# One layer's attention written out in a recorded order on all five engines, with the row minima of grouped-query attention scaled on ScalarE

## The chip, the cores and the metric

The kernel runs on one core of a Trainium2 chip. The metric is device time in microseconds (us) of one execution, from its first to its last instruction. The time before is 1951.8 us, the median of three runs (1947.15 to 1954.22).

## The reference

A two-layer diffusion backbone works on 512 latent and 256 context tokens of 1024 channels. Each layer normalises and modulates the tokens, projects them, attends in two branches, adds the gated branches, projects again, and ends with a SwiGLU feed-forward block. The part around the change is the attention:

```python
na_q, na_k, na_v, gq, gk, gv, ga, gb = jnp.split(h @ w_in[l], IN_SPLITS, axis=-1)
ya = merge_heads(na_latent(qa, ka, va, ka_c, va_c, bias, row_idx))   # 8 heads, 8x16 window + context
qb = apply_rope(rms_norm(heads(gq, GQA_Q_HEADS), q_gain[l]), cos, sin)   # 8 query heads
kb = apply_rope(rms_norm(heads(gk, GQA_KV_HEADS), k_gain[l]), cos, sin)  # 2 key heads
ob = gqa_latent(qb, k_all, v_all)     # softmax over 512 latent + 256 context keys
x = x + g1 * branch_merge(ya, yb, ga, gb, w_pa[l], w_pb[l], w_o[l])
if not last: ...                      # the context tokens' own queries, in layer 0 only
```

## The kernel before, in words

Every large product is done in full precision as three products of rounded halves: a weight or activation is cast to a high part on ScalarE (`wh`, L369) and its rest is taken on GpSimd or VectorE (`wl`, L371), and TensorE adds high x high, high x low and low x high in one PSUM bank (L384).

The attention of one layer is built by `mixing`. Its items are pairs of query blocks: per head two pairs of 128 queries, 16 pairs of grouped-query attention (`gqa_pair`) and then 16 of windowed attention (`na_pair`). For a grouped-query pair, TensorE writes the scores of two blocks into three PSUM banks (`sc`, L1040), VectorE takes each row's minimum (L1048; the scores carry a minus sign) and multiplies it by the query's inverse norm (L1054), ScalarE takes the exponential with that value as bias (`p`, L1056), VectorE divides by the row sums (L1009, L1010), TensorE transposes (`tp`, L1066), ScalarE and VectorE split the transposed block into halves (`pth` L1016, `ptl` L1017), and TensorE multiplies with the values (`y`, L1076), whose two partition halves are joined by ScalarE and VectorE (L1024, L1027). The scores have one set of three banks, the transposes and values three banks (`t`), the projections two (`g`). So the next pair's scores wait until this pair's exponentials have read theirs.

Between the items TensorE runs fillers: the projections of later heads, with their evacuation (`gqa_q`, `na_k`, `na_q`, `na_v`, `gate`). `Flow` plans this. It keeps a clock, books each evacuation or exponential on a line per engine (`go`, with fixed and per-element costs in `RATE`), and lets a filler run where an item would have to wait. The table `PLAN` holds one row of settings for each layer. What `Flow` decides is TensorE's order alone: the loop runs under a manual schedule for PE, and the order on VectorE, ScalarE, GpSimd and SyncE is set by the framework's scheduler.

Layer 1 starts its attention with the latent tokens while the context tokens are still being normalised (`late_norm`, `late_k`, `late_v`): the keys come in a latent part of 512 and a context part of 256 columns, and the first scores need both (`kk`, L1352 and L1353). GpSimd does the inverse norms (L807, a power), one product of the rotary embedding (L791), most of the `wl` and the windowed bias (L1491, L1492). SyncE loads the weights (L360) and moves query halves across partitions (L1001).

Of the kernel before, what the change touches and what calls it, by code (L numbers as in the profile page):

```python
# [44 lines left out]
for _n in ORDER:  # L45
    for _j in range(COLS[_n][1]):
# [32 lines left out]
         busy=12, ctx=0.0, vat=(1, 1), load=2, qt=2, rx=2, slow=(1.1, 1.2, 1), banks="gst", lead=(2, 1, 2), quiet=0.0, spared=0),  # L79
# [3 lines left out]
         busy=2, ctx=1, vat=(1, 1), load=2.5, qt=2, rx=1, slow=(1, 1, 1), banks="tsg", lead=(2, 2, 1), quiet=28.0, spared=2),  # L83
# [42 lines left out]


# [20 lines left out]
class Flow:  # L148
# [4 lines left out]
    def __init__(self, fillers, live, pace, hop, slow):  # L153
# [10 lines left out]

        self.rings = dict(g=[0.0] * 2, t=[0.0] * 3)
# [37 lines left out]
    def fill(self):  # L203
# [4 lines left out]
        if f.state == 0:  # L208
            next(f.steps)
# [4 lines left out]
        try:  # L214
            v = next(f.steps)
        except StopIteration:
# [8 lines left out]
        else:  # L225
            self.clock += v
# [5 lines left out]
    def ahead(self):  # L232

        for f in self.fillers:
            if f.state == 1:
                return
            if f.state == 0:
                next(f.steps)
                f.state = 1
                return  # L240

# [10 lines left out]
    def run(self, steps):  # L252
        mine = 0.0
        self.ahead()
        for v in steps:
            if isinstance(v, Until):
                self.wait(v.t)
            else:
                self.clock += v
# [8 lines left out]
    def force(self, ready):  # L268
        while not ready():
            if not self.fill():  # L270
                self.rest(self.clock + 0.5)

# [62 lines left out]
class Trunk:  # L335
    def __init__(self, tc, nc, dram):
        self.tc, self.nc, self.d = tc, nc, dram
# [12 lines left out]
    def ps(self, tag, n="ps", cols=512):  # L350
        if tag not in self.pbufs:
            tag = "a" if tag == "g" else "t" if "t" in self.pbufs else "n"
        return self.psum[tag].tile([P, cols], F32, tag=tag, bufs=self.pbufs[tag], name=self.name(n))
# [467 lines left out]
    def gqa_k(self, l, h, spans, pool, out):  # L821
# [25 lines left out]
        end = self.roped(flow.clock + 0.7)  # L847
        self.rope(kg, pool)
# [45 lines left out]
    def gqa_q(self, l, j, h, spans, pool, out):  # L894
# [14 lines left out]
        end = max(end, self.roped(flow.clock - 1.0))  # L909
        nr = self.small.tile([P, 16], F32, tag="hr", name=self.name("nr"))  # L910
        nc.vector.tensor_scalar(nr[:, : n // HD], r[:, : n // HD], -1.0, None, op0=ALU.mult)
        self.rope(qg, pool)
        yield Until(end - self.plan["soon"])
# [116 lines left out]
    def gqa_pair(self, head, q, kk, val, out, i, pool, done=None):  # L1030
# [20 lines left out]
        def exp(s, b, at):  # L1051
            m = ms[b]
            c = 2 * b + v
            nc.vector.tensor_tensor(m[:, 0:1], m[:, 0:1], r[:, c : c + 1], op=ALU.mult)  # L1054
# [4 lines left out]
            end = self.go(("v", 1), ("e", T), at=at)  # L1059
# [27 lines left out]
    def ctx_item(self, head, score, val, out, r, nr, v, pool, done):  # L1087
# [4 lines left out]
        def soft(s, at):  # L1092
# [3 lines left out]
            if r is not None:  # L1096
                rr = r[:].rearrange("p (t v) -> p v t", v=2)[:, v, 4:6]
                nc.vector.tensor_tensor(m[:, 0:2], m[:, 0:2], rr, op=ALU.mult)
            p = pool.tile([P, 512], F32, tag="p", name=self.name("p"))
            for b in range(2):  # L1100
# [4 lines left out]
                self.soften(p[:, c], m[:, 2 + b : 3 + b], pool)  # L1105
            ps_.append(p)
            end = self.go(("v", S), ("v", 1), ("e", 256), ("e", 256), at=at)
            return end, self.go(("v", 1), ("v", 1), ("w", 256), ("w", 256), at=end - 0.5)
# [45 lines left out]
    def na_pair(self, head, q, k, val, bias, out, i, pool, done=None):  # L1154
# [16 lines left out]
        def soft(s, b, at):  # L1171
# [7 lines left out]
                halves(z[:]), halves(s[:, 0:512]), add, 1.0, BIG, ALU.add, ALU.min, m[:, 0:1])  # L1179
            nc.scalar.activation(z, z, AF.Exp, bias=m[:, 0:1], scale=-1.0, accum_out=m[:, 1:2])  # L1180
            self.soften(z, m[:, 1:2], pool)
            zs.append(z)
            free = self.go(("v", S), at=at)
# [126 lines left out]
    def late_k(self, l, h, pool, out):  # L1310
# [7 lines left out]
        for a, b in ((0, S), (S, T)):  # L1318
# [22 lines left out]
            if a == 0:  # L1341
                end = self.roped(flow.clock + 0.7)
# [1015 lines left out]
```

## Time and profile before

| what | value |
|---|---|
| median of three runs | 1951.8 us (1947.15, 1951.8, 1954.22) |
| the profiled execution: its own time, its span | 1945.29 us, 1943.5 us |
| busy share of the span: PE, VectorE, ScalarE, GpSimd | 98%, 76%, 49%, 12% |
| mean granted TensorE clock | 0.998 |
| layer 0's attention, about 100 to 420 us | PE busy 316.8 of 320 us |
| layer 1's attention, about 1150 to 1400 us | PE busy 239.9, VectorE 196.4, ScalarE 153.4, GpSimd 67.2 of 250 us |

A row of the timeline gives the start, the time, the engine, the line, the operation with what it writes and reads, and in square brackets how long the engine stood idle before it and who ended that. PE is TensorE, DVE VectorE, ACT ScalarE, POOL GpSimd, SP SyncE. Busy time of PE overlaps from matmul to matmul, so its idle time is a little larger than what the busy share leaves.

### The profile page before, as it was taken

What the parts mean: (1) busy time and instruction counts of PE and PEld (TensorE: products, weight loads), DVE (VectorE), ACT (ScalarE), POOL (GpSimd) and SP (SyncE); (2) the same over time, 40 slices, a digit from 0 to 9 for tenths busy, and PEclk for the clock granted to TensorE, in tenths of its full rate; (3) what the DMA queues carried; (4) which work ended last, traced back from release to release, by engine and by line L of the source; (5) the groups of instructions that cost most, each with busy time, mean ns of one, the idle gap of its engine ahead of it and who ended that gap; (6) DMA issues with size and microseconds to landing.
All of it is one profiled execution on the core that took longest, in us unless ns stands there. A gap on an engine that the chain in (4) does not pass through costs nothing.

```text
span 1943.5 us, 31493 instructions
## 1 busy us (share of the span) xinstructions
PE 1912.1 (98%) x12298; PEld 1775.8 (91%) x12298; DVE 1470.0 (76%) x2802; ACT 943.0 (49%) x1822; POOL 226.6 (12%) x131
## 2 busy tenths in 40 slices
PE   8999999999999999999999998999999999999998
PEld 8989999998899999999999888889988999999998
DVE  7468887769877888786868577888657687877785
ACT  5466666652336533342424346666553355544553
POOL 0332222213300000000000012322300000000000
PEclk9999999999999999999999999999999999999999
DMA  8121112235562233334344411112235532332332
GB/s 328 44 65 48 47 64 63 77 105 182 170 217 87 66 120 122 117 116 133 131 141 143 143 62 55 47 60 64 73 102 173 201 109 77 98 120 88 103 97 83
DMA packets 71669, 210.85 MB, mean 108 GB/s; under 512 B 8544, under 2 KB 10720, under 8 KB 71520
## 3 DMA queue, kind: packets, MB, share of 16 engines
q1 hardware_dynamic: 71520, 208.84, 33.5%
q8 instruction: 96, 1.57, 0.3%
q14 instruction: 53, 0.43, 0.1%
HBM read 196.75 MB, written 6.82 MB: 105 GB/s over the span
## 4 chain that ended last, share of the span: by engine, by line
PE 69%; DVE 4%; issue 1%; ACT 1%; POOL 0%; DMA 0%; DVEq 0%; POOLq 0%; ACTq 0%
PE po L384 21%; PE qu L1740 14%; PE pj L384 11%; PE qv L1740 7%; PE pp L384 4%; PE qc L1740 3%; PE pf L384 3%; PE pv L957 1%; PE sc L1040 1%; PE y L1076 1%; PE tp L1066 1%; PE y L1203 1%; PE sc L1167 1%; PE tp L1191 1%; DVE m L1048 0%
## 5 line engine op out<-in xcount | busy, mean ns | idle before, releaser
L1740 PE MATMUL qu<-r,w 128*128 128x384 f32 (+1 forms) x1872 | 295.9, 310 | 0.3
L1740 PEld LDWEIGHTS qu<-r,w 128*128 128x128 f32 x1872 | 281.0, 190 | 4.9 <-DVE tt L2219 3.7
L384 PE MATMUL pj<-h,wh 128*128 128x512 f32 (+1 forms) x704 | 257.4, 366 | 3.3 <-ACT kg L816 1.7
L384 PE MATMUL pj<-h,wl 128*128 128x512 f32 (+1 forms) x704 | 247.6, 352 | 1.2 <-POOL wl L371 1.2
L384 PE MATMUL pj<-hl,wh 128*128 128x512 f32 (+1 forms) x704 | 247.0, 351 | 0.0
L369 ACT ACTIVATE wh<-wr 128x1024 fp32r<-128x1024 f32 (+1 forms) x131 | 124.6, 954 | 168.9 <-issue 43.5
L1603 ACT ACTIVATE w<-wr 128x512 fp32r<-128x512 f32 x234 | 145.4, 625 | 107.6 <-DVE wr L2183 36.1
L384 PE MATMUL po<-ph,wh 128*128 128x512 f32 (+1 forms) x576 | 197.5, 343 | 0.0
L384 PE MATMUL po<-ph,wl 128*128 128x512 f32 (+1 forms) x576 | 196.9, 342 | 0.0
L384 PE MATMUL po<-pl,wh 128*128 128x512 f32 (+1 forms) x576 | 196.3, 341 | 0.0
L371 POOL TENSOR_TENSOR wl<-wr,wh 128x1024 fp32r<-128x1024 f32 (+1 forms) x67 | 151.0, 2258 | 370.8 <-ACT wh L369 364.7
L1595 DVE SCALAR_TENSOR_TENSOR x<-po,G,x 128x256 f32<-128x256 f32 (+3 forms) x168 | 99.2, 596 | 101.0 <-PE po L384 100.0
L1607 DVE TENSOR_TENSOR w<-wr,w 128x512 fp32r<-128x512 f32 x234 | 159.4, 686 | 11.9 <-ACT w L1603 11.0
L384 PEld LDWEIGHTS pj<-h,wl 128*128 128x128 f32 x704 | 133.3, 189 | 19.7 <-POOL wl L371 1.6
L1740 PE MATMUL qv<-r,w 128*128 128x384 f32 (+1 forms) x936 | 150.7, 310 | 0.3 <-ACT tt L1746 0.3
L384 PEld LDWEIGHTS pj<-h,wh 128*128 128x128 f32 x704 | 133.7, 190 | 17.4 <-ACT kg L816 1.9
L384 PEld LDWEIGHTS pj<-hl,wh 128*128 128x128 f32 x704 | 134.0, 190 | 13.5
L1740 PEld LDWEIGHTS qv<-r,w 128*128 128x128 f32 x936 | 141.2, 190 | 0.5 <-ACT tt L1746 0.5
L1016 ACT ACTIVATE pth<-tp 128x512 fp32r<-128x512 f32 x176 | 103.2, 595 | 65.1 <-PE tp L1066 36.8
L512 POOL TENSOR_TENSOR rs<-rs,expo 128x2 f32<-128x2 f32 (+2 forms) x8 | 6.2, 773 | 1100.4 <-DVE rs L511 1100.4
L1017 DVE TENSOR_TENSOR ptl<-tp,pth 128x512 fp32r<-128x512 f32 x176 | 119.4, 684 | 18.4 <-ACT pth L1016 17.0
L384 PEld LDWEIGHTS po<-ph,wl 128*128 128x128 f32 x576 | 108.3, 188 | 14.3 <-DVE wl L1911 0.4
(255 smaller groups left out, 4325.2 us busy)
## 6 DMA issues: line engine op xcount, KB each, us to landing
wr<-wfi SPq DMA_DIRECT2D x88, 512.0 KB, 3.3
wr<-wmodT SPq DMA_DIRECT2D x84, 512.0 KB, 3.4
wr<-win SPq DMA_DIRECT2D x68, 512.0 KB, 3.3
wr<-wfo SPq DMA_DIRECT2D x64, 256.0 KB, 2.7
wr<-wo SPq DMA_DIRECT2D x26, 512.0 KB, 3.9
wr<-wp SPq DMA_DIRECT2D x32, 256.0 KB, 3.0
x<-x SPq DMA_DIRECT2D x16, 384.0 KB, 6.7
wr<-wmod SPq DMA_DIRECT2D x12, 512.0 KB, 7.6
```

The source lines that it names most:

```text
L369: nc.scalar.activation(hi, raw, AF.Copy)
L371: (eng or nc.gpsimd).tensor_tensor(lo, raw, hi[:].bitcast(F32), op=ALU.subtract)
L384: nc.tensor.matmul(ps[:, : b - a], u[:, c], v[k][:, a:b], start=(k == 0 and i == 0), stop=(k == nk - 1 and i == 2),)
L957: nc.tensor.matmul(ps[:, t * 256 : t * 256 + 256], a[k][:, tok], b[:, c], start=(k == 0 and i == 0), stop=(k == KB - 1 and i == 2))
L1016: nc.scalar.activation(hi, tp, AF.Copy)
L1017: nc.vector.tensor_tensor(lo, tp, hi[:].bitcast(F32), op=ALU.subtract)
L1040: nc.tensor.matmul(s[:, lo:up], qt[:, b * P : (b + 1) * P], kk[k][:, lo:up], start=(k == 0 and (b % 2 == 0 or lo > 0)), stop=(k == 1), ski ...
L1066: nc.tensor.transpose(tp[:, (2 * j + b) * P : (2 * j + b + 1) * P], ps_[b][:, (k + j) * P : (k + j + 1) * P], self.ident)
L1595: self.nc.vector.scalar_tensor_tensor(x[j][:, f:u], ps[:, f - a : u - a], self.G[l][i][:, s, j : j + 1], x[j][:, f:u], op0=ALU.mult, op1=A ...
L1603: self.nc.scalar.activation(t[:, :n], src, AF.Copy)
L1607: self.nc.vector.tensor_tensor(t[:, n : 2 * n], src, t[:, :n].bitcast(F32), op=ALU.subtract)
L1740: nc.tensor.matmul(banks[bank], u[:, c], v, start=(first and k == 0 and i == 0), stop=(k == kn - 1 and i == 2), skip_group_check=True)
```

## The change

The settings of layer 1 get `all=True`, those of layer 0 `all=False`. With `all`, every call that the attention of layer 1 makes on an engine is not issued but recorded (`Engines`, `Engine`, `Plan.add`): its engine, a cost by its shape (`Plan.cost`), the recorded instructions that it must follow (same bytes with a write among them, or the same PSUM bank from another engine), and a planned start and end. `Flow` then books nothing on its own lines but takes the ends from these records (`Plan.go`). When the whole attention is recorded, `Plan.emit` gives out all instructions in one order, under a manual schedule for all five engines. PE and SP keep the order in which they were recorded. On VectorE, ScalarE and GpSimd the next one is chosen among those that are ready, by when TensorE wants what comes of it (`due`), and a VectorE instruction between SBUF operands is not started while GpSimd runs (`shared`). Since the ends are other numbers, TensorE's own order in layer 1 changes too.

Two edits hold for both layers. The product of the row minimum and the inverse norm moves from VectorE to ScalarE: 32 products of one column in each layer in `gqa_pair`, and in layer 0's eight grouped context items one VectorE instruction of two columns becomes two on ScalarE. Layer 0's order on TensorE and elsewhere changes with it, under the old scheduler. The diff, cut:

```diff
@@ PLAN, layer 0 and layer 1
-         busy=12, ctx=0.0, vat=(1, 1), load=2, ..., quiet=0.0, spared=0),
+         busy=12, ctx=0.0, vat=(1, 1), load=2, ..., quiet=0.0, spared=0, all=False),
-         busy=2, ctx=1, vat=(1, 1), load=2.5, ..., quiet=28.0, spared=2),
+         busy=2, ctx=1, vat=(1, 1), load=2.5, ..., quiet=28.0, spared=2, all=True),
@@ Flow
     def go(self, t, *ops):
+        if self.plan:
+            return self.plan.go(t, ops)
...
+    def passed(self, v):
+        self.clock = max(self.clock + v, self.plan.pe if self.plan else 0.0)
+class Plan:
+    HOPS = dict(p=0.055, v=0.035, a=0.035, g=0.078, s=0.1)
+    TAIL = dict(p=-0.16, v=0.085, a=0.105, g=0.07, s=-2.2)
...
+    def cost(self, lane, op, aps, kw, psum):
...
+        if lane == "g":
+            return 0.31 if op == "memset" else 0.5 + n * 0.142 if n <= 16 else 0.14 + n * 0.0022
+        if lane == "a":
+            return 0.16 + n * 0.00088 + 0.08 * scaled + 0.1 * ("accum_out" in kw)
...
+    def emit(self):
...
+        for i in reversed(range(n)):
+            o = ops[i]
+            due[i] = o["at"] if o["lane"] == "p" else min(
+                [due[j] - o["cost"] - 0.05 for j in then[i] + frees[i]], default=o["at"] + 15.0)
...
+        queue = {e: [i for i, o in enumerate(ops) if o["lane"] == e] for e in "ps"}
...
+        def begins(i):
...
+            return max(t, clock["g"] - 0.07) if ops[i]["shared"] else t
...
+                if e == "g":
+                    times = [(put_off(i, t), i) for t, i in times]
+                if times:
+                    first = min(times)[0]
+                    d, t, i = min((due[i], t, i) for t, i in times if t <= first + 0.1)
...
+            if e == "a" and o["kw"].get("accum_out") is not None and not exp:
+                exp = True
+                clock[e] += 1.28
+                end[i] += 1.28
...
+        for i in sorted(range(n), key=lambda i: (start[i], i)):
+            ops[i]["run"](*ops[i]["args"], **ops[i]["kw"])
@@ gqa_pair
-            nc.vector.tensor_tensor(m[:, 0:1], m[:, 0:1], r[:, c : c + 1], op=ALU.mult)
+            nc.scalar.activation(m[:, 0:1], m[:, 0:1], AF.Copy, scale=r[:, c : c + 1])
...
-            end = self.go(("v", 1), ("e", T), at=at)
+            end = self.go(("a", 1), ("e", T), at=at)
@@ ctx_item
-                nc.vector.tensor_tensor(m[:, 0:2], m[:, 0:2], rr, op=ALU.mult)
+                for b in range(2):
+                    nc.scalar.activation(m[:, b : b + 1], m[:, b : b + 1], AF.Copy, scale=rr[:, b : b + 1])
@@ mixing
-            with tc.manual_schedule(engines={mybir.EngineType.PE}):
+            if PLAN[l]["all"]:
+                nc.plan = flow.plan = Plan(flow)
                 flow.run(self.attend(items))
+                nc.plan = None
+                every = ("PE", "DVE", "Activation", "Pool", "SP")
+                with tc.manual_schedule(engines={getattr(mybir.EngineType, e) for e in every}):
+                    flow.plan.emit()
+            else:
+                with tc.manual_schedule(engines={mybir.EngineType.PE}):
+                    flow.run(self.attend(items))
```

Beside these, `put_off` delays a GpSimd instruction behind a VectorE one that is about to be ready and due sooner, the calls that book the rotary embedding are replaced by the recorded end, and a recorded instruction keeps the ring of buffers that the tile pools use.

In the rows below every instruction of layer 1's attention of the kernel after carries line L541, where `Plan.emit` gives it out. The first place is VectorE where the first pair's scores become ready. `kk` are the halves of the keys, `v` those of the values, `qg` a later query head in its rotary embedding, `m` the minima (TENSOR_REDUCE), `hr` the inverse norms. Before:

```order
L790 STREAM_SHUFFLE sh_12272<-qg_12114 128x512
L892 TENSOR_TENSOR v_11837<-tv_12157,v_11837 128x2x64
L1353 TENSOR_TENSOR kk_11970<-kg_11714,kk_11969 64x256 x2
L792 TENSOR_TENSOR qg_12114<-qg_12114,cos_sb 128x512
L1353 TENSOR_TENSOR kk_11976<-kg_11714,kk_11975 64x256 x2
L892 TENSOR_TENSOR v_11838<-tv_12157,v_11838 128x2x64
L793 TENSOR_TENSOR qg_12114<-qg_12114,sh_12272 128x512
L1048 TENSOR_REDUCE m_12207<-sc_12198 128x1
L1048 TENSOR_REDUCE m_12209<-sc_12198 128x1
L1054 TENSOR_TENSOR m_12207<-m_12207,hr_11824 128x1
L1054 TENSOR_TENSOR m_12209<-m_12209,hr_11824 128x1
```

After:

```order
L541 STREAM_SHUFFLE sh_11910<-qg_11867 128x512
L541 TENSOR_TENSOR kk_11855<-kg_11722,kk_11854 64x256 x2
L541 TENSOR_TENSOR v_11819<-tv_11875,v_11819 128x2x64
L541 TENSOR_TENSOR v_11820<-tv_11875,v_11820 128x2x64
L541 TENSOR_REDUCE m_11881<-sc_11880 128x1
L541 TENSOR_REDUCE m_11882<-sc_11880 128x1
L541 TENSOR_TENSOR qg_11867<-qg_11867,cos_sb 128x512
L541 TENSOR_TENSOR qg_11867<-qg_11867,sh_11910 128x512
L541 TENSOR_TENSOR kk_11857<-kg_11722,kk_11856 64x256 x2
```

The two pieces of the second key head (`kk` with the higher number, which the first scores do not read) and the query's rotary embedding (`qg`) stood ahead of the minima and now stand behind them; the two products of the minima have left VectorE.

The second place is ScalarE at the same point: the halves, the first minima and exponentials of the attention (`p`), the cast of a weight (`wh`) and evacuations of values (`v`). Before:

```order
L891 ACTIVATE v_11837<-tv_12157 128x2x64
L1352 ACTIVATE kk_11969<-kg_11714 64x256 x2
L1352 ACTIVATE kk_11975<-kg_11714 64x256 x2
L891 ACTIVATE v_11838<-tv_12157 128x2x64
L1056 ACT_TABLE_LOAD
L1056 ACTIVATE p_12212,m_12207<-sc_12198,m_12207,nr_11827 128x768
L966 ACTIVATE v_12250<-pv_12176 128x2x64
L1056 ACTIVATE p_12218,m_12209<-sc_12198,m_12209,nr_11827 128x768
```

After:

```order
L541 ACTIVATE kk_11854<-kg_11722 64x256 x2
L541 ACTIVATE v_11819<-tv_11875 128x2x64
L541 ACTIVATE wh_11877<-wr_11876 128x1024
L541 ACTIVATE v_11820<-tv_11875 128x2x64
L541 ACTIVATE kk_11856<-kg_11722 64x256 x2
L541 ACTIVATE m_11881<-m_11881,hr_11815 128x1
L541 ACTIVATE m_11882<-m_11882,hr_11815 128x1
L541 ACT_TABLE_LOAD
L541 ACTIVATE p_11883,m_11881<-sc_11880,m_11881,nr_11816 128x768
L541 ACTIVATE p_11885,m_11882<-sc_11880,m_11882,nr_11816 128x768
L541 ACTIVATE v_11887<-pv_11879 128x2x64
```

Both products of minima stand on ScalarE in front of the first exponential, one behind the other, and the two exponentials follow without an evacuation between them. A little earlier on ScalarE (not shown) the evacuation of the context keys' projection (`sq`, `kg`, L815 and L816) stood behind the cast of a second weight, and now stands ahead of it.

The third place is VectorE in the twelfth of the sixteen grouped-query pairs. `k` is a windowed key's half, `ptl` the halves of transposed blocks, `rc` and `p` the division by the row sums, `y` the join of a value product. Before:

```order
L1017 TENSOR_TENSOR ptl_13250<-tp_13244,pth_13249 128x512
L936 TENSOR_TENSOR k_13321<-pj_13168,k_13321 64x512
L1048 TENSOR_REDUCE m_13271<-sc_13262 128x1
L1048 TENSOR_REDUCE m_13273<-sc_13262 128x1
L936 TENSOR_TENSOR k_13324<-pj_13168,k_13324 64x512
L1054 TENSOR_TENSOR m_13271<-m_13271,hr_12267 128x1
L1017 TENSOR_TENSOR ptl_13293<-tp_13287,pth_13292 128x512
L1054 TENSOR_TENSOR m_13273<-m_13273,hr_12267 128x1
L1027 TENSOR_TENSOR y_13221<-y_13296,ys_13309 64x256
L1017 TENSOR_TENSOR ptl_13318<-tp_13312,pth_13317 128x512
```

After:

```order
L541 TENSOR_TENSOR ptl_12094<-tp_12092,pth_12093 128x512
L541 TENSOR_TENSOR ptl_12103<-tp_12101,pth_12102 128x512
L541 TENSOR_REDUCE m_12105<-sc_12104 128x1
L541 TENSOR_TENSOR ptl_12113<-tp_12111,pth_12112 128x512
L541 TENSOR_REDUCE m_12106<-sc_12104 128x1
L541 RECIPROCAL rc_12108<-m_12105 128x1
L541 TENSOR_SCALAR p_12107<-p_12107,rc_12108 128x768
L541 RECIPROCAL rc_12110<-m_12106 128x1
L541 TENSOR_SCALAR p_12109<-p_12109,rc_12110 128x768
L541 TENSOR_TENSOR y_12091<-y_12114,ys_12115 64x256
L541 TENSOR_TENSOR ptl_12118<-tp_12116,pth_12117 128x512
```

Before, both minima and two windowed key halves stood between one half of a transposed block and the next; now a half stands between the two minima, and no key half in this stretch.

More of the change, by code (lines that the diff above doesn't have):

```diff
@@ L82 @@
          early=0.8, reserve=2, hop=0.2, move=3, soon=0, keep=2,
-         busy=2, ctx=1, vat=(1, 1), load=2.5, qt=2, rx=1, slow=(1, 1, 1), banks="tsg", lead=(2, 2, 1), quiet=28.0, spared=2),
+         busy=2, ctx=1, vat=(1, 1), load=2.5, qt=2, rx=1, slow=(1, 1, 1), banks="tsg", lead=(2, 2, 1), quiet=28.0, spared=2, all=True),
 ]
@@ L908, in gqa_q @@
         end = self.go(("p", n // HD), at=t)
-        end = max(end, self.roped(flow.clock - 1.0))
+        if not flow.plan:
+            end = max(end, self.roped(flow.clock - 1.0))
         nr = self.small.tile([P, 16], F32, tag="hr", name=self.name("nr"))
@@ L912, in gqa_q @@
         self.rope(qg, pool)
+        if flow.plan:
+            end = max(end, self.go(("v", S), at=flow.clock))
         yield Until(end - self.plan["soon"])
```

245 lines of the change are left out of this document (228 added, 17 removed).

## The prediction

> **What bounds the kernel now.** I read the page first, then the busy time of each engine by stage, then the waits of TensorE inside the stage that is reordered, then the timelines around the longest of them.
>
> ```profile
> span 1943.5 us, 31493 instructions
> PE 1912.1 (98%) x12298; PEld 1775.8 (91%) x12298; DVE 1470.0 (76%) x2802; ACT 943.0 (49%) x1822; POOL 226.6 (12%) x131
> ```
>
> TensorE is the bound, and its work stays the same, matmul for matmul. All that another order can give is its idle time. By stage (time, then busy time of PE, PEld, DVE, ACT, POOL, granted clock):
>
> ```profile
> 100.00:420.00 320.00, 316.82 (x2216) 292.67 (x2215) 246.60 (x567) 200.54 (x442) 78.41 (x43) 1.00 0.22 67
> 1150.00:1400.00 250.00, 239.89 (x1627) 217.72 (x1626) 196.36 (x437) 153.41 (x317) 67.24 (x39) 0.99 0.18 56
> ```
>
> Layer 1's attention (second row) leaves 250 - 239.9 = 10.1 us, layer 0's 3.2 us. VectorE is at 196.4 of 250 us, 79%: not the bound, but full enough that what it does first matters. TensorE's waits in that stage (in total, times, longest):
>
> ```profile
> PE sc L1040 <- ACT p L1056: 2.0, 2, 1.7
> PE tp L1066 <- DVE ptl L1017: 1.9, 1, 1.9
> PE pj L384 <- ACT kg L816: 1.7, 1, 1.7
> PE sc L1040 <- DVE kk L1353: 1.4, 1, 1.4
> PE y L1076 <- DVE ptl L1017: 1.0, 2, 0.8
> PE tp L1066 <- DVE p L1010: 0.8, 1, 0.8
> PE st L804 <- DVE y L1027: 0.7, 1, 0.7
> PE y L1203 <- DVE ptl L1017: 0.4, 1, 0.4
> PE pj L384 <- DVE ql L991: 0.2, 1, 0.2
> ```
>
> They are few and long, they add up to the 10.1 us, and most end on VectorE. One of them costs more than itself:
>
> ```profile
> 1284.69 0.66 PE L1066 MATMUL tp<-ident_sb,p 128*128 128x128 f32 x4 [1.91 <-DVE ptl L1017]
> 1280.00:1290.00 10.00, 8.09 (x53) 7.61 (x52) 8.07 (x16) 4.71 (x9) 0.00 (x0) 0.83 0.07 16
> ```
>
> After 1.91 us of idling the granted clock is 0.83 over these ten microseconds: (1 - 0.83) x 10 = 1.7 us of matmul time lost. So the most that the stage can give back is 10.1 + 1.7 = 11.8 us, 0.6% of the run.
>
> **The change, part by part.** *First scores (sc <- kk, 1.4).* VectorE there:
>
> ```profile
> 1184.64 2.23 DVE L1353 TENSOR_TENSOR kk<-kg,kk 64x256 fp32r<-64x256 f32 x2
> 1186.91 0.69 DVE L792 TENSOR_TENSOR qg<-qg,cos_sb 128x512 f32<-128x512 f32 x1
> 1187.63 0.87 DVE L1353 TENSOR_TENSOR kk<-kg,kk 64x256 fp32r<-64x256 f32 x2
> 1188.53 0.29 DVE L892 TENSOR_TENSOR v<-tv,v 128x128 fp32r<-128x128 f32 x1
> 1188.74 0.68 DVE L793 TENSOR_TENSOR qg<-qg,sh 128x512 f32<-128x512 f32 x1
> 1189.34 1.81 DVE L1048 TENSOR_REDUCE m<-sc 128x1 f32<-128x768 f32 x2
> ```
>
> Two key halves took 2.23 us where the next two took 0.87: 1.4 us of standing. That VectorE stands while GpSimd runs is seen in the clear later on:
>
> ```profile
> 1344.10 2.39 POOL L371 TENSOR_TENSOR wl<-wr,wh 128x1024 fp32r<-128x1024 f32 x1 [9.63 <-ACT wh L369]
> 1345.23 1.55 DVE L1010 TENSOR_SCALAR z<-z,rc 128x512 f32<-128x512 f32 x1
> 1347.48 0.49 DVE L1010 TENSOR_SCALAR z<-z,rc 128x512 f32<-128x512 f32 x1
> ```
>
> The same instruction takes 0.49 us alone and 1.55 us when it starts inside GpSimd's, ending just behind it. The new order plans around this and puts the pieces straight behind the shuffle. But in its own new order TensorE comes to these scores after 15 matmuls of the value projection instead of 21, so sooner, and I leave 0.5 of the wait: 0.9 us gained (0 to 1.4).
>
> *Second scores (sc <- p, 1.7 of the 2.0).* They need the three score banks, so minima, exponentials and what lies between. The minima began at 1189.34, behind the second key head, a `v` and the embedding's products: 0.69 + 0.87 + 0.68 = 2.2 us, which the new order moves behind them. The minima can't start before the scores end, and the `v` pieces stay ahead, so not all of that arrives. The rest of the chain stays, with this in it:
>
> ```profile
> 1191.30 1.28 ACT L1056 ACT_TABLE_LOAD   x1 [5.45 <-DVE m L1054]
> ```
>
> It stands behind the minima in the new order too. I take 0.7 us (0 to 1.3).
>
> *Context keys' bank (pj <- kg, 1.7).*
>
> ```profile
> 1170.65 1.06 ACT L369 ACTIVATE wh<-wr 128x1024 fp32r<-128x1024 f32 x1 [1.22 <-PE pj L384]
> 1171.61 0.37 ACT L815 ACTIVATE sq<-pj 128x256 f32<-128x256 f32 x1
> 1171.87 0.47 ACT L816 ACTIVATE kg<-pj,gain_sb 128x256 f32<-128x256 f32 x1
> ```
>
> The cast `wh` delays the evacuation by its 1.06 us; it now stands behind. The evacuation's own 0.37 + 0.47 can't go, so at most 1.7 - 0.84 = 0.9; other evacuations are woven in, and I take 0.5 (0 to 0.9).
>
> *The pair loop (1.9, 0.8 of `y`, 0.8, 0.7, the small ones 0.3 + 0.2 + 0.4 + 0.2).* The longest, before 1284.69:
>
> ```profile
> 1276.17 2.43 DVE L919 TENSOR_TENSOR q<-qg,q 64x512 fp32r<-64x512 f32 x2
> 1280.45 0.69 DVE L936 TENSOR_TENSOR k<-pj,k 64x512 fp32r<-64x512 f32 x1
> 1281.17 1.82 DVE L1048 TENSOR_REDUCE m<-sc 128x1 f32<-128x768 f32 x2
> 1283.94 0.69 DVE L1017 TENSOR_TENSOR ptl<-tp,pth 128x512 fp32r<-128x512 f32 x1
> ```
>
> `ptl`, which frees the bank that TensorE wants, is behind a key half needed much later and two minima (0.69 + 1.82), and VectorE is late besides by a standstill in `q`. The new order has `ptl` between the minima and no key half there. The four long waits are 1.9 + 0.8 + 0.8 + 0.7 = 4.2; I take two thirds, 2.8 (1 to 4.2), since VectorE stays 76% busy or more and some half will still come late. Of the small ones, 1.1 in all, I take 0.4. What is late next is the same thing with less lead: a `ptl` or the exponential for the next scores.
>
> *The clock.* The 1.7 us go if the 1.91 us wait goes: I take 1.2 (0 to 1.7). The Trainium skill (TensorE: Matmul & The Clock Gate, HAM oscillation) has the clock fall only on idle gaps above about 3.4 us. Here it fell after 1.91 us, and the measurement decides; by the page this term would be 0 and the sum 1.2 less.
>
> *The minima on ScalarE.* No such instruction is in the trace. Its nearest rows, of one column and of the smallest evacuation, beside the one removed (layer 1, then layer 0) and the reduction in front:
>
> ```profile
> L1056 ACT ACTIVATION_READ_ACCUMULATOR p<-sc,m,nr 128x1 f32 x32 | 6.2, 193 | 0.0
> L990 ACT ACTIVATE qh<-pj 64x64 fp32r<-64x64 f32 x6 | 1.3, 214 | 0.9 <-DVE ql L991 0.9
> L1054 DVE TENSOR_TENSOR m<-m,hr 128x1 f32<-128x1 f32 x32 | 5.5, 182 | 0.1
> L1054 DVE TENSOR_TENSOR m<-m,hr 128x1 f32<-128x1 f32 x30 | 10.4, 353 | 0.0
> L1048 DVE TENSOR_REDUCE m<-sc 128x1 f32<-128x768 f32 x32 | 29.3, 951 | 7.1 <-PE sc L1040 6.7
> ```
>
> 32 x 0.21 = 6.8 us more on ScalarE in layer 1, which has 97 us free there, and 5.5 us less on VectorE: nothing on the path either way. In layer 0 VectorE sheds more (353 ns each, with standstills in them), but there TensorE is idle for 3.2 us only, and its order moves for small reasons: 0, between -1.5 and +1.5.
>
> *New waits.* A plan is not the run; where a duration differs, engines that keep their order wait. 1.0 us lost (0 to 4), by the small waits of the list.
>
> Sum: 0.9 + 0.7 + 0.5 + 2.8 + 0.4 + 1.2 - 1.0 = 5.5 us. The profiled execution, 1945.3 us, would become 1939.8. It lies 6.5 us under the median of the runs shown; taken off that median, 1951.8 - 5.5 = **1946.3 us**. A measurement of this kernel can tell about 0.5%, 9.8 us, so this is "within 0.5%".
>
> **The rivals.** *All of it goes.* The waits are few, each has its cause in the order, and the costs in the planner match the rows (a cast remainder on GpSimd 2.39 us, a table load 1.28). Then 10.1 + 1.7, and 1.0 of layer 0's: 12.8 us, 1939.0. Against it: the table load and the evacuation stay on the path.
>
> *The waits move and do not go*, so that the change doesn't do what it is planned to. TensorE's order is new too, and the single set of score banks holds each pair to its own chain; then 1951.8. For it: the chain minima, exponentials, scores is long. Against it: only two of sixteen pairs wait for `p`.
>
> *Minima dearer on ScalarE.* Two of 0.214 us in front of each first exponential, with no credit for VectorE's, are 0.43 us a pair; in 13 of the pairs of layer 1 they eat the 5.5 us: 1951.8. The Trainium skill (ScalarE: Activation LUTs, Rules for kernel authors) wants a multiplication on VectorE. By that page's figure (What ACT_TABLE_LOAD costs: 186 ns, and 93 more for a pointer operand) I estimate 0.56 us a pair.
>
> *Slower: ScalarE held by the second minimum.* Its two products stand one behind the other ahead of the first exponential, and ScalarE takes nothing out of order. The second waits for a reduction of 0.95 us, and the casts and `pth` queued behind wait with it, which TensorE's transposes need. At 0.95 us in 20 of the 32 pairs of both layers, 19.0 us: 1951.8 - 5.5 + 19.0 = 1965.3. It decides from (9.8 + 5.5) / 0.95, some 17 pairs, on. Against it: VectorE's own order gave the first exponential no earlier start before, since both products stood behind both reductions there too.
>
> **How the numbers follow.** Forecast 0.55, all of it 0.20, moved 0.07, dearer minima 0.06, ScalarE held 0.12. The forecast's own bounds run from 3 us lost (1 of the pair loop against 4 of new waits) to 10.6 gained (all upper ends); 0.04 of its 0.55 lies beyond 9.8. Faster by over 0.5%: 0.20 + 0.04 = 0.24. Slower: 0.12. Within: 0.64. The range takes in "all of it" with layer 0's half microsecond more, and the two cases at 1951.8 with the upper end of the new waits, 4 us: 1938 to 1956. It leaves out the slower case and a little on either side.
>
> **What would show it.** Right: in the profile after, idle time of PE in layer 1's attention near 5 us, no long `tp <- ptl`, no half-clock stretch, a wait of about 1 us at the second scores, VectorE rows of `kk`, `q` and `z` at their undisturbed times. Wrong: `p` as the releaser of `sc` in many pairs, ScalarE idle in front of `m`, new idles near 2 us with a fallen clock behind them, or a PE idle time in layer 0 that grew by more than 1.5 us.

## The result, and the profile after

The kernel after takes 1968.3 us (median of four runs, 1964.8 to 1972.2) beside 1949.5 us for the kernel before (four runs, 1944.2 to 1954.2): a ratio of 1.0097, 95% interval 1.0067 to 1.0126. It is slower by 18.9 us, where 5.5 us less were forecast.

The page of the profiled execution after. TensorE's busy time is 7.5 us longer for the same number of matmuls, its idle time 46.8 us instead of 31.4:

```profile
span 1966.4 us, 31465 instructions
PE 1919.6 (98%) x12298; PEld 1777.6 (90%) x12298; DVE 1464.0 (74%) x2730; ACT 960.4 (49%) x1902; POOL 226.8 (12%) x131
```

The stages after (time, busy time of PE, PEld, DVE, ACT, POOL, clock):

```profile
100.00:420.00 320.00, 315.57 (x2200) 290.41 (x2200) 234.33 (x527) 208.43 (x484) 79.56 (x43) 1.00 0.21 65
1150.00:1420.00 270.00, 252.14 (x1680) 226.37 (x1679) 203.00 (x419) 164.73 (x355) 67.21 (x38) 0.99 0.17 53
```

Layer 1's attention now leaves 17.9 us of 270 (before 10.1 of 250), layer 0's 4.4 of 320 (before 3.2). TensorE's waits in layer 1's attention after:

```profile
PE sc L541 <- DVE m L541: 9.4, 10, 1.1
PE sc L541 <- ACT p L541: 2.6, 6, 0.8
PE pj L541 <- ACT kg L541: 2.3, 1, 2.3
PE tp L541 <- DVE z L541: 2.0, 2, 1.4
PE sc L541 <- DVE kk L541: 0.9, 1, 0.9
PE tp L541 <- DVE p L541: 0.7, 1, 0.7
```

The list ends at 1420 us. From there to the end of the stage two more follow, 1.2 us for `z` and 0.2 us for `m`.

The waits for `ptl` and `y` of before are gone. The first row was not there before at all: ten times, 0.8 to 1.05 us each, scores wait for the minimum `m`, which reads scores. Five of the ten are in grouped-query pairs. The timeline of one:

```profile
1202.96 1.45 PE L541 MATMUL sc<-kk,q 128*128 128x512 f32 x7
...
1204.44 0.96 DVE L541 TENSOR_REDUCE m<-sc 128x1 f32<-128x768 f32 x1 [0.32 <-PE sc L541]
1205.43 0.29 ACT L541 ACTIVATE m<-m,hr 128x1 f32<-128x1 f32 x1 [0.91 <-DVE m L541]
...
1205.45 0.50 PE L541 MATMUL sc<-kk,q 128*128 128x512 f32 x1 [1.05 <-DVE m L541]
...
1205.99 0.96 DVE L541 TENSOR_REDUCE m<-sc 128x1 f32<-128x768 f32 x1 [0.59 <-PE sc L541]
```

Seven of the pair's eight score matmuls run, then VectorE reduces the first block, and the eighth matmul, which writes the second block, starts only when that reduction has ended. The other five waits are in windowed pairs, where the last matmuls of the second block wait in the same way:

```profile
1361.68 0.61 PE L541 MATMUL sc<-k,ql 128*128 128x128 f32 x3 [0.79 <-DVE m L541]
```

Behind the wait at 1205.45 us follows a half-clock stretch (granted clock 0.83 over these ten microseconds, again 1.7 us lost):

```profile
1200.00:1210.00 10.00, 8.95 (x58) 8.38 (x57) 7.27 (x17) 7.93 (x18) 1.64 (x1) 0.83 0.01 2
```

The program's order says why. TensorE's last score matmuls of a grouped-query tile with their semaphore waits, two in the kernel before (pair two) and the last in after (pair two):

```
5771 L1040 MATMUL sc_12287<-kk_11969,q_11921 128x512
5772 L1040 MATMUL sc_12287<-kk_11970,q_11921 128x512
...
5757 L541 MATMUL sc_11893<-kk_11855,q_11834 128x512 [waits DVE_49]
```

The two blocks of a pair share one tile of three banks: block one fills columns 0 to 768, block two the rest, its last 512 columns being the third bank. `Plan.add` compares banks, so for the plan that last matmul and the first reduction have nothing to do with each other. `Plan.emit` issues instructions by planned start, so the reduction comes ahead of the matmul in the program, and the program that is built from that sequence makes the matmul wait for it. Before, the same matmul carries no wait, and both reductions stood behind all of a pair's scores. Why the built program makes a matmul wait for a reduction of the tile's other banks was not followed further; that the order of issue brings the wait, and takes it away, the third experiment shows.

The stages in all profiled executions. Layer 1's attention is counted from the start of the first score matmul to the start of the first `pp` matmul (before 1184.81 to 1452.09, after 1194.12 to 1474.97; `pp` is the first product behind the attention), layer 0's likewise; "output" is layer 0's output product, from the first `po` to the first `pf` matmul, with which the feed-forward block begins. The ratio compares a kernel with before, measured beside it. The medians of before in these comparisons run from 1948.1 to 1951.2 us, so a difference of 2 or 3 us between the medians of two rows says little.

| kernel | layer 0 attention | output | layer 1 attention | median, ratio to before [95%] |
|---|---|---|---|---|
| before | 334.1 | 67.9 | 267.3 | 1948.1 to 1951.2 |
| after | 336.9 | 74.7 | 280.9 | 1968.3, 1.0097 [1.0067, 1.0126] |
| layer 0's minima back | 334.0 | 73.4 | 280.0 | 1963.8, 1.0064 [1.0048, 1.0080] |
| no plan | 338.3 | 73.7 | 269.0 | 1956.5, 1.0031 [1.0019, 1.0044] |
| reductions behind scores | 338.3 | 68.8 | 269.4 | 1957.8, 1.0034 [1.0020, 1.0049] |
| plan alone | 334.1 | 73.2 | 290.4 | 1975.1, 1.0124 [1.0108, 1.0140] |
| both undone | 335.5 | 72.6 | 268.5 | 1954.9, 1.0019 [1.0005, 1.0034] |
| the same, VectorE minima | 334.0 | 72.7 | 273.7 | 1959.3, 1.0054 [1.0041, 1.0068] |
| the same, layer 0's minima on ScalarE, old order | 335.7 | 72.7 | 268.7 | 1952.5, 1.0020 [1.0008, 1.0031] |
| both undone, TensorE's old order | 334.2 | 72.3 | 266.9 | 1952.0, 1.0021 [1.0010, 1.0033] |
| the same, loads freed | 335.8 | 74.3 | 258.8 | 1942.6, 0.9969 [0.9957, 0.9981] |
| both undone, loads freed | 334.1 | 72.5 | 264.4 | 1948.4, 0.9998 [0.9985, 1.0010] |
| both undone, standstills not counted | 335.5 | 74.5 | 271.8 | 1955.7, 1.0038 [1.0023, 1.0052] |
| loads freed, layer 0 recorded too | 332.7 | 73.5 | 257.0 | 1945.9, 0.9985 [0.9972, 0.9998] |

The column of layer 0 holds a clock term. Layer 0's attention takes 334.0 to 334.2 us in six executions in which its instructions are those of before, and 335.5 to 335.8 us in three others with the same instructions. In both undone, one of the three, the granted clock is 0.83 from 170 to 180 us, a loss of 1.7 us; with layer 0's minima back it is 1.00 there. The two rows of 338.3 have such a stretch too (0.87 and 0.83), and after, with the same layer 0, has none (1.00).

The column of the output product misleads. The two profiles differ by 6.8 us in the output product, and the kernel with layer 0's minima back, whose layer 0 is that of before instruction for instruction, shows 5.5 of them too (its waits of TensorE there):

```profile
PE po L656 <- DVE wl L643: 3.0, 2, 2.8
PE po L656 <- ACT mh L1887: 0.2, 1, 0.2
```

So this is the execution, not the change: the profile of before, 1945.3 us, is a quick one without that wait. In the profile after the chain behind it begins at a transfer:

```profile
553.33 1.23 DVE L724 CUSTOM_DVE_ANT_0 junk<-wr,crow 128x1024 f32<-128x1024 f32 x1 [4.05 <-DMA wr<-wmodT]
...
555.76 0.44 PE L656 MATMUL po<-mh,wl 128*128 128x384 f32 x1 [2.75 <-DVE wl L643]
```

What the change itself does stands in the other two columns: 13.6 us in layer 1's attention and 2.8 us in layer 0's.

Of the 13.6 us, 9.0 are idle time of TensorE (17.2 against 8.2 us in the stage) and 4.6 are busy time (263.7 against 259.0 us), at the same loss to the clock, 1.7 us in each. Part of the busy time belongs to the waits as well. In a row of matmuls of 512 columns one starts 0.23 us behind another; ahead of a wait one holds TensorE for 0.40 us, and behind it for 0.34 us (1231.55 to 1231.89 in the profile after). By these figures a wait costs about 0.27 us beside its idle time, and the 13 more waits of the stage (22 against 9) about 3.5 us, an estimate. Six more matmuls now start behind the first score instead of ahead of it, which is about the rest.

### The profile page after: what moved, and what is told of

Read it like the earlier page. It is cut to its first block, busy times and chain, and to the rows that moved or that the text cites. A ratio compares the mean times of both kernels' runs of the same rounds, so it can differ in the third digit from the quotient of the medians.

```text
span 1966.4 us, 31465 instructions
## 1 busy us (share of the span) xinstructions
PE 1919.6 (98%) x12298; PEld 1777.6 (90%) x12298; DVE 1464.0 (74%) x2730; ACT 960.4 (49%) x1902; POOL 226.8 (12%) x131
## 4 chain that ended last, share of the span: by engine, by line
PE 62%; DVE 7%; ACT 2%; issue 2%; DMA 1%; POOL 0%; SPq 0%; DVEq 0%; POOLq 0%; ACTq 0%
PE po L656 20%; PE qu L2036 13%; PE qv L2036 7%; PE pj L541 4%; PE pj L656 4%; PE qc L2036 3%; PE pf L656 3%; PE pp L656 2%; PE pv L541 2%; PE sc L541 1%; PE y L541 1%; PE tp L541 1%; DVE m L541 1%; DVE z L541 1%; ACT p L541 1%
## 5 line engine op out<-in xcount | busy, mean ns | idle before, releaser
L656 PE MATMUL pj<-h,wh 128*128 128x512 f32 (+1 forms) x512 | 182.3, 356 | 1.8 <-DVE t L1883 0.9
L656 PE MATMUL pj<-h,wl 128*128 128x512 f32 (+1 forms) x512 | 176.8, 345 | 1.0 <-POOL wl L643 1.0
L656 PE MATMUL pj<-hl,wh 128*128 128x512 f32 (+1 forms) x512 | 176.7, 345 | 0.0
L641 ACT ACTIVATE wh<-wr 128x1024 fp32r<-128x1024 f32 (+1 forms) x109 | 101.4, 933 | 135.0 <-PE po L656 30.4
L643 POOL TENSOR_TENSOR wl<-wr,wh 128x1024 fp32r<-128x1024 f32 (+1 forms) x47 | 102.4, 2182 | 247.5 <-ACT wh L641 247.2
L656 PEld LDWEIGHTS po<-pl,wh 128*128 128x128 f32 x576 | 108.5, 188 | 12.8
L656 PEld LDWEIGHTS po<-ph,wh 128*128 128x128 f32 x576 | 108.5, 188 | 12.8
L724 DVE CUSTOM_DVE_ANT_0 wr<-wr,crow 128x1024 f32<-128x1024 f32 x80 | 101.4, 1268 | 13.4 <-DMA wr<-wmodT 13.0
L656 PEld LDWEIGHTS pj<-h,wl 128*128 128x128 f32 x512 | 96.8, 189 | 13.4 <-POOL wl L643 1.4
L656 PEld LDWEIGHTS pj<-h,wh 128*128 128x128 f32 x512 | 97.0, 189 | 12.8 <-issue 1.1
```

What stands on the lines that cost most here:

```text
L641: nc.scalar.activation(hi, raw, AF.Copy)
L643: (eng or nc.gpsimd).tensor_tensor(lo, raw, hi[:].bitcast(F32), op=ALU.subtract)
L656: nc.tensor.matmul(ps[:, : b - a], u[:, c], v[k][:, a:b], start=(k == 0 and i == 0), stop=(k == nk - 1 and i == 2),)
L724: self.nc.vector.tensor_tensor_reduce(junk if s else w, w, crow[:, s], 1.0, 0.0, ALU.mult, ALU.add, self.mod[l][:, s, n : n + 1])
```

## The experiments

Mine: layer 1 loses by score matmuls that wait for a reduction issued ahead of them, and layer 0 by its moved minima. The rivals: ScalarE held by the second minimum (the slower rival of the prediction), the recorded order in itself, and, for layer 0, chance.

**Layer 0's minima back on VectorE.**

```diff
-            nc.scalar.activation(m[:, 0:1], m[:, 0:1], AF.Copy, scale=r[:, c : c + 1])
+            if self.flow.plan:
+                nc.scalar.activation(m[:, 0:1], m[:, 0:1], AF.Copy, scale=r[:, c : c + 1])
+            else:
+                nc.vector.tensor_tensor(m[:, 0:1], m[:, 0:1], r[:, c : c + 1], op=ALU.mult)
```

> Kernel after, with layer 0's minima (pairs and context items) multiplied on VectorE again; layer 1 as in after. Mine: layer 0 loses through the moved minima, so the first score of layer 1 comes at 1184.8 us as before (after: 1194.1), layer 1's attention from the first score to the last transposed pair stays at 280 us, total about 1958.6 (after 1968.3 - 9.7). Rival 'ScalarE held' and rival 'order itself' say nothing on layer 0. Rival 'layer 0's loss is chance of one execution': total about 1963 to 1968, first score of layer 1 within 3 us of the after's.

Measured 1963.8 us, in the rival's range. Layer 0's attention went back to 334.0 us; the output product did not (above). My theory of layer 0 was more than half wrong: of the 9.3 us by which the first score of layer 1 comes later in the profile after (1194.1 against 1184.8), 6.8 are the output product. The intervals of the two ratios, after's and this one's, overlap, so for layer 0 the stage in the profiles is the better evidence.

**No plan, minima on ScalarE in both layers.**

```diff
-         ... quiet=28.0, spared=2, all=True),
+         ... quiet=28.0, spared=2, all=False),
```

> The minima on ScalarE in both layers, layer 1 not recorded (old scheduler). Mine: layer 0 loses its 9.7 us as in after, layer 1's attention as before (267 us), total about 1959 (before 1949.5 + 9.7). Rival 'ScalarE held by the second minimum': layer 1 loses here too, 0.95 us in most of 16 pairs, 10 us or more: about 1970. Rival 'chance': 1950.

Measured 1956.5 us. Layer 1 stays at 269.0 us, 1.7 more than before, so minima on ScalarE do not cost 0.95 us in most pairs: the slower rival falls. (TensorE's order in layer 1 shifts here too, since the minima are booked on another line.) Layer 0 has 338.3 us, after's 336.9 and 1.4 more, with the half-clock stretch named above.

**Reductions behind the scores.** In `Plan.emit`, a reader of a score tile gets an output key no earlier than the last score matmul that precedes it there:

```diff
-        for i in sorted(range(n), key=lambda i: (start[i], i)):
+        out = list(start)
+        for t, users in self.users.items():
+            if t in rings and rings[t][1] == "s":
+                last = 0.0
+                for u in users:
+                    if ops[u]["lane"] == "p":
+                        last = max(last, start[u])
+                    else:
+                        out[u] = max(out[u], last)
+        for i in sorted(range(n), key=lambda i: (out[i], i)):
```

> Kernel after; in the recorded order the instructions that read a score tile are given out behind the last score matmul that comes before them in TensorE's order, so that no matmul waits for the reduction of the pair's first block. Mine: the waits of score matmuls for the minima (9.4 us in 10) and the half clock of 1.7 us behind them go: layer 1's attention about 269 us, total 1957 to 1959. Rival 'ScalarE held': gain under 2 us, 1966 to 1968. Rival 'order itself': waits reappear at the next release (exponentials, evacuations), gain 0 to 4, total 1964 to 1968.

Measured 1957.8 us, 10.5 less than after where the rivals had 4 at most, and layer 1's attention 269.4 us, as forecast. By operation, tile and shape, the order of instructions in the stage is the same as in after on TensorE, VectorE, ScalarE and GpSimd alike (1737 matmuls, 422 instructions on VectorE), so what the edit changes is when instructions wait and not who goes first. The row of ten waits is gone, and what is left is a little more than before had (waits of TensorE in layer 1's attention up to 1420 us; one of 1.4 us for `z` follows):

```profile
PE sc L550 <- ACT p L550: 4.4, 7, 0.9
PE tp L550 <- DVE z L550: 2.2, 2, 1.4
PE pj L550 <- ACT kg L550: 2.3, 1, 2.3
PE sc L550 <- DVE kk L550: 0.9, 1, 0.9
PE tp L550 <- DVE p L550: 0.5, 1, 0.5
```

**Plan alone, minima on VectorE in both layers** (the edit of the first experiment without its condition).

> Kernel after with the minima multiplied on VectorE in both layers (recorded order alone). Mine: layer 0 as before (gain 9.7), layer 1 still with the waits of score matmuls for the reductions: 276 to 281 us there, total 1955 to 1959. Rival 'ScalarE held by the second minimum': layer 1's attention back to 267 to 270 us, total 1945 to 1949. Rival 'order itself': as mine.

Measured 1975.1 us: slower than after, against all three theories. The longest waits of TensorE in layer 1's attention, and its product of the minima (time in all, mean ns) in the pair loop:

```profile
PE sc L541 <- DVE m L541: 11.9, 12, 1.4
PE sc L541 <- ACT p L541: 5.5, 3, 2.3
```

```profile
L541 DVE TENSOR_TENSOR m<-m,hr 128x1 f32<-128x1 f32 x32 | 7.3, 259 | 0.0
```

With layer 0 equal, it lies 11.3 us over the kernel with layer 0's minima back (1975.1 - 1963.8), and 10.4 in layer 1's attention. The plan, and TensorE's order with it, is made anew when the product moves, so this compares two plans and not one instruction: 7.0 of the 10.4 us are idle time and 3.4 are two more half-clock stretches. With this planner the product belongs on ScalarE.

**Both undone.** The first and the third experiment together.

> Kernel after with both suspected costs taken out: layer 0's minima on VectorE, and the readers of a score tile given out behind the score matmuls that come before them. Mine: layer 0's attention 334 us as before, layer 1's 269.4 us against 267.3 before, total 2 us over before. If the two add up from the first four kernels: 1951 + 6.6 (reductions behind scores) - 4.6 (layer 0's minima) = 1953. Rival 'chance': about 1957 as with the reductions alone.

**The same with layer 1's minima on VectorE.**

> As the kernel with both undone, but layer 1's minima on VectorE too. Rival 'ScalarE held by the second minimum': layer 1's attention gains here, 264 to 267 us, total 1947 to 1950. Mine: the minima on ScalarE are no loss in layer 1, where the recorded order put the plan alone 10 us behind; the attention takes 270 to 276 us, total 1954 to 1960.

**The same as both undone, with layer 0's pair minima on ScalarE but booked as before**, so that TensorE's order in layer 0 stays.

> As the kernel with both undone, but layer 0's 32 pair minima are multiplied on ScalarE while the bookings and so TensorE's order in layer 0 stay as before. If the instructions on ScalarE cost layer 0 its 3 to 4 us: its attention takes 337 to 338 us, total 1956 to 1957. If the shifted order of TensorE in layer 0 costs them: 334 us, total 1953, as with both undone.

Both undone measured 1954.9 us, between my forecast and the rival's 1957: together the two edits take 13.4 us off after (4.6 and 10.5 alone), and layer 1's attention is 268.5 us. With VectorE's minima 1959.3, 4.4 more, and no grouped score waits for a minimum: minima on ScalarE are no loss in layer 1 under this planner, and the rival falls here too. (TensorE's order is again another.) The third, 1952.5 us, can't be told from both undone by its time; its profile has layer 0's attention at 335.7 us without a half-clock stretch, 1.6 more than with VectorE's minima, and one wait of 1.6 us for an inverse norm. So in that execution the pair products alone cost about 1.6 of the 2.8 us; whether the rest is TensorE's shifted order or the context items' products stays open. Where one wait arises shows in the profile after:

```profile
169.28 1.82 DVE L1327 TENSOR_REDUCE m<-sc 128x1 f32<-128x768 f32 x2
171.13 0.95 DVE L1198 TENSOR_TENSOR q<-qg,q 64x768 fp32r<-64x768 f32 x1
...
172.11 1.29 DVE L1296 TENSOR_TENSOR ptl<-tp,pth 128x512 fp32r<-128x512 f32 x2
...
172.95 0.95 PE L1355 MATMUL y<-pth,v 128*128 128x256 f32 x6 [1.75 <-DVE ptl L1296]
```

and at the same place before, with a `ptl` between the two reductions:

```profile
170.46 0.94 DVE L1048 TENSOR_REDUCE m<-sc 128x1 f32<-128x768 f32 x1
...
171.43 0.69 DVE L1017 TENSOR_TENSOR ptl<-tp,pth 128x512 fp32r<-128x512 f32 x1
172.04 0.95 DVE L1048 TENSOR_REDUCE m<-sc 128x1 f32<-128x768 f32 x1
...
172.27 0.95 PE L1076 MATMUL y<-pth,v 128*128 128x256 f32 x6 [0.58 <-DVE ptl L1017]
```

**TensorE's old order.** What both undone still has over before must come from TensorE's own new order or from the other engines'. Here `Flow` books on its own lines as before and only the other engines follow the record:

```diff
-                nc.plan = flow.plan = Plan(flow)
+                nc.plan = rec = Plan(flow)
...
-            end = flow.lines[lane].take(t, cost - self.TAIL[lane]) + self.TAIL[lane]
+            end = self.lines[lane].take(t, cost - self.TAIL[lane]) + self.TAIL[lane]
```

> As the kernel with both undone, but TensorE's order in layer 1 is the one of before, instruction for instruction; VectorE, ScalarE and GpSimd follow the recorded order planned around it. If the waits that are left (11.7 us in layer 1) come from TensorE's new order: layer 1's attention 262 to 266 us, total 1946 to 1950. If they come from the new order on the other engines: 269 to 275 us, total 1953 to 1959.

Measured 1952.0 us, layer 1's attention 266.9, between the two cases. TensorE's 1731 matmuls of the stage come in the order of before. But one wait of TensorE was 4.5 us long and another 2.1, each for `m` of a windowed pair. The first, followed back:

```profile
1314.39 0.30 POOL L551 MEMSET bias<- 128x256 f32 x1
...
1330.02 0.33 SPq L551 DMA_DIRECT2D yd<-y  x1
1330.45 0.87 SPq L551 DMA_DIRECT2D bias<-rpb  x2
...
1333.79 1.80 POOL L551 TENSOR_TENSOR bias<-bias 128x768 f32<-128x768 f32 x1 [19.09 <-DMA bias<-rpb]
1335.62 0.69 DVE L551 CUSTOM_DVE_ANT_1 z<-sc,bias 128x512 f32<-128x512 f32 x1 [1.67 <-POOL bias L551]
...
1337.08 0.61 PE L551 MATMUL sc<-k,qh 128*128 128x256 f32 x2 [4.48 <-DVE m L551]
```

GpSimd cleared the bias buffer at 1314.4, but its load was issued at 1330.5: on SyncE it stood behind the store `yd`, which waits for a finished `y`. SyncE keeps the recorded order in this plan. The next experiment tests whether that order is the cause.

**Loads freed.** Weight and bias loads keep their order among themselves, moves and stores theirs, and the plan takes whichever is ready:

```diff
                 some = queue[e][:1] if e in queue else can[e]
+                if e == "s":
+                    some = [next(k, None) for k in (
+                        (i for i in queue[e] if store(i)), (i for i in queue[e] if not store(i)))]
+                    some = [i for i in some if i is not None]
```

> As the kernel with TensorE's old order, but on SyncE the loads of weights and bias no longer keep their recorded place behind moves and stores that wait for late data; both kinds keep their order among themselves. Mine: the two waits of windowed scores (4.5 and 2.1 us) came from bias loads held on SyncE's queue, and go: layer 1's attention 260 to 262 us, total 1944 to 1947. Rival: the bias is late through GpSimd's own order: 266 to 267 us, total 1952.

> As the kernel with both undone (TensorE's new order), with the loads freed on SyncE in the same way. Mine: its own waits are not for the bias (one of 6.5 us on VectorE did not reach TensorE), so within 2 us of it: layer 1's attention 266 to 269 us, total 1952 to 1955. Rival 'SyncE's order is what the recorded plan lacks everywhere': 260 to 263 us, total 1947.

With TensorE's old order 1942.6 us: faster than both kernels (0.9969, 0.9957 to 0.9981), layer 1's attention 258.8 us, less than I had expected. Both waits for `m` are gone, and the rival of GpSimd's own order with them. Its waits of TensorE there, all of them:

```profile
PE pj L558 <- ACT kg L558: 1.5, 1, 1.5
PE st L558 <- DVE y L558: 1.2, 1, 1.2
PE sc L558 <- ACT p L558: 0.4, 1, 0.4
PE sc L558 <- DVE kk L558: 0.4, 1, 0.4
```

3.5 us where before had 10.1. With TensorE's new order 1948.4 us and 264.4, between my expectation and the rival's: SyncE's order cost 4.1 us there too (268.5 to 264.4), which I had not expected. The rest against the old order is 5.6 us. The two largest rows:

```profile
PE sc L557 <- ACT p L557: 4.3, 7, 1.1
PE pj L557 <- ACT kg L557: 2.3, 1, 2.3
```

Seven times TensorE stands at its scores until an exponential has freed their banks: 4.3 us where the old order has 0.4. The wait for `kg` lies ahead of the first score and is not part of the 5.6 us. Why `Flow` with the recorded ends puts them there was not tried.

**Standstills not counted.** `begins` returns `t` and `put_off` is not asked.

> As the kernel with both undone, but the plan no longer holds VectorE's SBUF instructions back while GpSimd runs, nor GpSimd's behind VectorE's. If counting the standstills pays: layer 1's attention 270 to 275 us, total 1956 to 1960. If it only moves waits: 266 to 269 us, total 1953 to 1955.

Measured 1955.7 us, layer 1 271.8 us beside 268.5. The bounds of its ratio overlap those of both undone, and the 3.3 us in layer 1 are about what a longer half-clock stretch there takes (clock 0.66 from 1345 to 1355 us, 3.4 us). So what counting GpSimd's standstills is worth stays open; it is not the cause of the loss.

**Layer 0 recorded too.** On top of the loads freed with TensorE's old order, `all=True` for layer 0.

> As the kernel with the loads freed and TensorE's old order, with layer 0's attention recorded in the same way too (pair minima on ScalarE there, context items' on VectorE). TensorE waits 4.2 us there in before. Mine: the recorded order takes most of them away and the minima cost nothing once their place is planned: layer 0's attention 330 to 332 us, total 1938 to 1941. Rival 'minima on ScalarE cost layer 0': 336 to 338 us, total 1945 to 1948.

Measured 1945.9 us. Layer 0's attention is shorter, 332.7 us against 334.1 without a half-clock stretch, with the pair minima on ScalarE. (TensorE's waits there in before add up to 3.5 us, not the 4.2 of the expectation.) The gain is lost again in front of it, by a new wait in the projections ahead of the first scores, at 93.8 us, and a half-clock stretch behind it (clock 0.83 from 90 to 100 us):

```profile
PE pv L558 <- DVE v L558: 2.6, 1, 2.6
```

## Why the prediction was wrong, point by point

- **New waits, 1.0 us (0 to 4): the step that failed.** Up to 1420 us they are 9.4 us for `m`, 2.0 for `z`, 2.6 for `p` in front of scores and 0.7 for `p` in front of transposes: 14.7 us, and 1.4 more by the end of the stage. I treated the plan's order as harmless except where durations drift. The 9.4 us are no drift: they are semaphore waits that the new order of issue puts into the program, and with the same order on every engine and the reductions issued behind the scores they are gone, and 11.5 us of layer 1's attention with them, 1.7 of these the half-clock stretch. The list of waits that TensorE's instructions carry, before beside after, shows them without any time.
- **Pair loop, 2.8 gained.** Right as far as it goes, and more: the four long waits, 4.2 us, are gone, and the small ones too. What came instead is booked above.
- **First scores, 0.9.** 1.4 became 0.9, so 0.5 gained. VectorE still stands (two key halves take 1.84 us, where the next two took 0.87 before), and GpSimd started 0.12 us behind it:

```profile
1193.91 1.84 DVE L541 TENSOR_TENSOR kk<-kg,kk 64x256 fp32r<-64x256 f32 x2
1194.03 1.45 POOL L541 TENSOR_TENSOR sh<-sh,sin_sb 128x512 f32<-128x512 f32 x1 [3.14 <-DVE sh L541]
```

- **Second scores, 0.7.** 1.7 became nothing: the second pair's scores start at 1202.96 us without idle time in front, and the first wait for `p` comes at 1260.66 us. I had left 1.0 of it.
- **Context keys' bank, 0.5.** 1.7 became 2.3: the wrong way. The cast does stand behind the evacuation, but a query piece `qh` that waits for `ql` has taken its place:

```profile
1181.34 0.63 DVE L541 SCALAR_TENSOR_TENSOR ql<-pj,qh 64x448 fp32r<-64x448 f32 x1
1182.00 0.22 ACT L541 ACTIVATE qh<-pj 64x64 fp32r<-64x64 f32 x1 [0.45 <-DVE ql L541]
...
1182.24 0.47 ACT L541 ACTIVATE kg<-pj,gain_sb 128x256 f32<-128x256 f32 x1
```

- **Clock, 1.2 gained.** The old stretch went, one like it came at 1205.8 us: nothing gained.
- **Minima on ScalarE, 0.** In layer 1 wrong on the good side with the recorded order: the plan made for ScalarE's minima is 4.4 us (both undone) to 11.3 us faster than the one made for VectorE's. Under the old scheduler it is the other way, 1.7 us more in layer 1 (no plan). Each product takes 0.29 us against VectorE's 0.18 before and 0.26 in the plan alone. The Trainium skill (ScalarE: Activation LUTs, Rules for kernel authors) would have it on VectorE; with the recorded order the dearer engine is the better one here.
- **Layer 0, 0 (-1.5 to 1.5).** 2.8 us in the profile, 4.6 us by medians (1968.3 against 1963.8): outside the bounds, since I judged by TensorE's idle time there and not by what VectorE's order does when the products leave it.
- **The base.** That the profiled execution lies 6.5 us under the median was said, and was needed: its output product is 4.4 to 6.8 us shorter than in all but one of the others.
- **The slower rival** has 1965.3 us, near the result, for a reason that the runs reject, so its nearness is luck: what costs the time is TensorE held by VectorE's reduction, and not ScalarE. Of my signs of being wrong, `p` in front of `sc` (six times) came true, and ScalarE idle in front of `m` (15 times, 13.0 us). The second misleads: with the reductions behind the scores ScalarE idles there for 16.6 us, and the kernel is 10.5 us faster. Idle time in layer 0 grew by 1.2 us (3.2 to 4.4), short of the 1.5 that I had named. That a reduction could hold TensorE was not among the signs.

The rest of the idea was sound: the waits of before were in the order's power. With reductions behind scores, layer 0's minima back, TensorE's old order and loads freed, 8.5 us of layer 1's attention go (267.3 to 258.8), of the 11.8 that I called the most.

## What to carry to other kernels

A written-out order decides not only who goes first but which semaphore waits the program gets: list the waits of the bounding engine in the program before and after, and look for those that the plan's own rules don't know. An in-order queue that takes loads and late stores in one sequence can hold a load for 16 us (1314.4 to 1330.5 here); freeing the loads took 8.1 us off the stage. And look first at the stages that the edit can't touch: two executions of the same instructions differed here by 5.5 us in one of them (67.9 and 73.4).

## What the runs showed of the hardware

The same wait, 2.3 us for `kg`, in the same order of instructions, is followed by a half-clock stretch in one execution and by none in the other. Both undone, the wait, and the ten microseconds around it by engine:

```profile
1178.39 0.38 PE L550 MATMUL pj<-h,wh 128*128 128x256 f32 x1 [2.34 <-ACT kg L550]
```

```profile
1178.00:1188.00 10.00, 9.61 (x59) 8.66 (x60) 7.59 (x9) 3.09 (x5) 6.20 (x3) 1.00 0.41 134
```

The kernel with layer 0's minima on ScalarE in the old order:

```profile
1180.23 0.58 PE L550 MATMUL pj<-h,wh 128*128 128x256 f32 x1 [2.35 <-ACT kg L550]
```

```profile
1178.00:1188.00 10.00, 7.77 (x41) 7.26 (x42) 7.85 (x10) 3.93 (x8) 4.84 (x3) 0.83 0.52 159
```

So in these runs the length of one wait does not decide it, and a term for the clock has an uncertainty of its own, 1.7 us for a stretch and 3.4 for the longest (1345 to 1355 us with standstills not counted). The Trainium skill (TensorE: Matmul & The Clock Gate, HAM oscillation) names gaps above about 3.4 us; here one of 2.35 us was enough and one of 2.34 us was not.
